# New durations in the planner that spreads side jobs over a stream of matrix products

## The chip, the core and the metric

The kernel runs on one core of a Trainium2 chip, in one launch. The metric is the device time of that launch in microseconds. A core has a matrix engine (PE, its weight loads shown apart as PEld), a vector engine (DVE), an activation engine (ACT), a general engine (POOL) and a queue engine (SP) that here only issues DMAs. Each engine works its own instructions in the order in which they stand in its queue, and waits on the others through semaphores.

## The reference, cut to what matters

Two transformer-like blocks over 256 tokens of width 2048, everything in float32. The first has a gated attention of 8 heads with forget gates, and an RWKV-7 recurrence of 16 heads; the second a gated causal convolution, a latent attention with rotary positions of 16 heads, and an attention over 256 memory tokens.

```python
h = rmsnorm(x); u = h @ w_in                      # 2048 -> 12488 columns
o_a = fox_attention(q, k, v, log_f) * silu(z_a)   # 8 heads of 128
o_b = (groupnorm(rwkv7_scan(r, decay, k, v, kk, kk*a)) + bonus) * silu(z_b)
m = sigmoid(g_a) * (o_a @ w_proj_fox) + sigmoid(g_b) * (o_b @ w_proj_rwkv)
x = rmsnorm(x + m @ w_out)
p = rms_norm(x) @ w_in_2                          # second block
o_conv = (b_gate * causal_conv(c_gate * u)) * silu(conv_z) @ w_conv_out
o_mla  = (mla_attention(c_q, c_kv, k_rope) * silu(mla_z)) @ w_mla_out
o_mem  = (memory_attention(mem_q, mem) * silu(mem_z)) @ w_mem_out
out = x + (sigmoid(g_conv)*o_conv + sigmoid(g_mla)*o_mla + sigmoid(g_mem)*o_mem) @ w_o
```

## The kernel before, in words

All large products are written as one stream, group by group: lora, r, kr, vr, fq, fk, fv, fz, zb, then ga with pf, gb, pr, wo for the first block; mk, mv, cq, ckv, krope, mq, mz, the heads' qr, qn, kn, kv, the convolution's cg, cu, cb, cz, then gm with mo, gc with co, lz, gl with lo and w2 for the second. Weights come as blocks of 128 x 1024 float32 through SP's queue. `conv_to` (L399) splits each block: ACT rounds it to a high part (whi), DVE subtracts to get a low part (wlo). Each product is then made of three matmuls: high by high, high by low, low by high. There are 4 buffers for raw blocks and 4 for each part.

A group is either channel-major (the matmul has 256 columns, four accumulators) or token-major (512 columns, two accumulators, `tm=True`). `gemm` (L472) goes through a group in rounds of two blocks; at the head of a round it writes the conversion of two further blocks. A channel-major round is 48 matmuls, a token-major one 24. Accumulators lie in 5 PSUM banks, and the last product of an accumulator is followed by its evacuation.

Everything else is a side job: a Python generator that writes some instructions and yields. `pump` (L459) is called four times in a round, after 12 matmuls of 256 columns or 6 of 512. It lets each of the first three waiting jobs take a step, or up to six steps where the job yields SOFT, as long as the planner doesn't hold DVE or ACT for too busy. For that the helpers keep three clocks, in estimated microseconds: `mm` adds to the clock of PE, `tt`, `ts`, `stt` and others to that of DVE, `act` to that of ACT. A job isn't stepped while DVE's or ACT's clock is over 1.5 us ahead of PE's:

```python
return max(clock["dve"], clock["act"]) > clock["pe"] + pace['m']
```

nor before PE's clock has reached the end of what the job wrote last on DVE or ACT (`Job.waits`, L431). `lag` (L436) holds a job for 5 us of PE's clock, or twice that, while a transfer goes through DRAM: `head_rs` (L597) writes the 8 or 4 rows of a normalisation to DRAM (hd) and reads them back spread over the partitions (hr). `finish` (L447) steps named jobs to their end where their result is needed, whatever the clocks say.

Side jobs that matter here: `rwkv_job` (L819), twice, the second behind the first. It computes the inverse of a triangular matrix by a loop of 31 steps (L956), each a product TM and a sum into W on DVE, whose sizes rise from 31 to 256 elements and fall again; before it a matrix goes through DRAM (Ld, then W1), behind it one comes back as XA, which the matmuls u read. Its last stage scales CE with hr. `fox_job` (L1147), twice, is four attention heads in turn: scores fs, softmax, transposes fpt, products fo. Both of these must be done ahead of ga (`finish(*jf)`, L1226); the RWKV jobs ahead of pr. `mla_job` is the latent attention's heads.

The program is built with `tile.TileContext(nc, schedule_with_timeline_sim=True)`: the order on each engine is laid out when the program is built, so that what is written is not always run in the written order.

Of the kernel before, what the change touches and what calls it, by code (L numbers as in the profile page):

```python
# [11 lines left out]
F32R = mybir.dt.float32r  # L12
# [215 lines left out]
def hybrid_kernel(ctx: ExitStack, tc: tile.TileContext, io, out):  # L228
# [3 lines left out]
    clock = {"pe": 0.0, "dve": 0.0, "act": 0.0}  # L232

    def fsz(ap):
        n = 1
        for s in ap.shape[1:]:
            n *= s
        return n
# [44 lines left out]

    def mm(o, l, r, start=True, stop=True):
        n = fsz(o)
        clock["pe"] += max(0.000424 * n, 0.0001 + 0.0016 * fsz(l) / 2) if l.dtype == F32R else max(0.00168 * n, 0.00168 * fsz(l))
        TE.matmul(o, lhsT=l, rhs=r, start=start, stop=stop)  # L287


# [182 lines left out]
    def gemm(name, pairs, evac):  # L472
# [4 lines left out]
        for b0 in range(0, e["nb"], step):  # L477
# [9 lines left out]
            if e["tm"]:  # L487
                for t in range(2):
                    for b, i, k in ks:
                        wh = hi_t[b][:, i * cols:(i + 1) * cols]  # L490
                        wl = lo_t[b][:, i * cols:(i + 1) * cols]
                        ah = pairs[k // 4][0][:, k % 4, 128 * t:128 * t + 128]
                        al = pairs[k // 4][1][:, k % 4, 128 * t:128 * t + 128]
                        mm(acc[t], ah, wh, start=k == 0, stop=False)
                        mm(acc[t], ah, wl, start=False, stop=False)
                        mm(acc[t], al, wh, start=False, stop=k == kt - 1)
                        if i == per - 1:
                            pump()
                    if ks[-1][2] == kt - 1:
                        evac(t, acc[t])  # L500
            else:
                for c in range(nt):
                    o = acc[c][:, :256]
                    for b, i, k in ks:
                        s = i * cols + 128 * c
                        wh, wl = hi_t[b][:, s:s + 128], lo_t[b][:, s:s + 128]
                        ah, al = pairs[k // 4][0][:, k % 4, :], pairs[k // 4][1][:, k % 4, :]
                        mm(o, wh, ah, start=k == 0, stop=False)
                        mm(o, wh, al, start=False, stop=False)
                        mm(o, wl, ah, start=False, stop=k == kt - 1)  # L510
                    if ks[-1][2] == kt - 1:
                        evac(c, o)
                    pump()
# [1221 lines left out]

MARGIN, SLACK = (1.5, 0), (1.5, 1)
MAXJOBS, NSTEP = 3, 6
CD, CA = 0.065, 0.17
LAG, HOP = 5, 0.0
SOFT = 1  # L1740

# [31 lines left out]
```

## Time and profile before

| | |
|---|---|
| time, median of 3 runs | 2058.05 us (2056.01 to 2065.45) |
| time of the profiled execution | 2055.2 us |
| its span, first to last instruction | 2053.4 us |
| PE busy | 2021.0 us, 98%, 13456 matmuls |
| DVE busy | 1304.9 us, 64%, 1987 instructions |
| ACT busy | 968.3 us, 47%, 1334 instructions |
| POOL busy | 73.9 us, 133 instructions |
| mean granted clock | 0.996 |
| DMA | 374.97 MB, 183 GB/s |

Times of the trace count from the span's start. Matmuls are pipelined: one of 256 columns lasts 0.28 us in the trace while the next starts 0.12 us after it, so its cost is the distance between starts. The granted clock of a stretch is a share of full speed; TensorE runs at one of two levels, 2.4 GHz and half of it, so a stretch at 0.8 has spent two fifths at the lower one.

### The profile page before, as it was taken

Reading aid. Unit: us, or ns where it says so; the run is one execution under the profiler, and the core shown is the slowest. Engines: PE = TensorE matmul, PEld = TensorE weight load, DVE = VectorE, ACT = ScalarE, POOL = GpSimd, SP = SyncE. Lnnn points to the kernel's source line nnn. Section 1 sums busy time; section 2 is a strip of 40 time slices with the busy share of each in tenths; the row PEclk is TensorE's granted clock in tenths of the full one; section 3 lists DMA queues with packets and bytes.
Section 4 is the critical chain, followed back from the end, with each engine's and each line's share of the span. In section 5 each row is a group of like instructions: output and inputs, shape, how many; then the busy total and the mean of one; then the engine's idle time right before and its main releaser. Section 6 shows DMA issues by size and latency. Waiting matters only on the chain.

```text
span 2053.4 us, 33342 instructions
## 1 busy us (share of the span) xinstructions
PE 2021.0 (98%) x13456; PEld 1822.4 (89%) x13456; DVE 1304.9 (64%) x1987; ACT 968.3 (47%) x1334; POOL 73.9 (4%) x133
## 2 busy tenths in 40 slices
PE   8999999998998999999999999999999999999999
PEld 8999989897777888898999999998888889988887
DVE  8776737868446478666865776755755655555554
ACT  6634435444444445554554435445545444444442
POOL 0002000020000000000000000000000000000000
PEclk9999999999999999999999999999999999999999
DMA  7555644544546656665555554556655555566564
GB/s 248 172 182 166 199 131 135 175 134 156 171 155 217 213 191 211 194 209 185 193 188 182 157 175 154 196 164 193 207 185 176 193 172 179 195 212 201 192 195 154
DMA packets 105674, 374.97 MB, mean 183 GB/s; under 512 B 12920, under 2 KB 13904, under 8 KB 105520
## 3 DMA queue, kind: packets, MB, share of 16 engines
q1 hardware_dynamic: 97568, 350.73, 52.8%
q0 software_dynamic: 7952, 22.12, 3.7%
q8 instruction: 105, 1.72, 0.3%
q14 instruction: 49, 0.40, 0.1%
HBM read 365.76 MB, written 5.86 MB: 181 GB/s over the span
## 4 chain that ended last, share of the span: by engine, by line
PE 94%; DMA 2%; DVE 2%; issue 1%; ACT 1%; POOL 0%; SPq 0%; DVEq 0%; ACTq 0%; POOLq 0%
PE acc.lz L287 4%; PE acc.ga L287 4%; PE acc.gb L287 4%; PE acc.gl L287 4%; PE acc.wo L287 4%; PE acc.w L287 4%; PE acc.lo L287 4%; PE acc.gc L287 4%; PE acc.gm L287 4%; PE acc.fq L287 2%; PE acc.r L287 2%; PE acc.zb L287 2%; PE acc.mz L287 2%; PE acc.mq L287 2%; PE acc.fk L287 2%; PE acc.mk L287 2%
## 5 line engine op out<-in xcount | busy, mean ns | idle before, releaser
L242 DVE TENSOR_TENSOR wlo<-raw,whi 128x1024 fp32r<-128x1024 f32 (+1 forms) x659 | 795.7, 1221 | 540.1 <-ACT whi L279 529.9
L279 ACT ACTIVATE whi<-raw 128x1024 fp32r<-128x1024 f32 (+1 forms) x659 | 683.1, 1055 | 757.3 <-issue 88.1
L287 PE MATMUL acc.lz<-h2h,whi 128*128 128x256 f32 x256 | 72.6, 284 | 0.0
L287 PE MATMUL acc.lz<-h2l,whi 128*128 128x256 f32 x256 | 72.6, 284 | 0.0
L287 PE MATMUL acc.lz<-h2h,wlo 128*128 128x256 f32 x256 | 72.5, 283 | 0.0
L287 PE MATMUL acc.gb<-wlo,hh 128*128 128x512 f32 x128 | 50.5, 398 | 6.0 <-DVE wlo L242 6.0
L287 PE MATMUL acc.ga<-whi,hh 128*128 128x512 f32 x128 | 50.9, 402 | 4.5 <-DVE zb L262 4.5
L287 PE MATMUL acc.ga<-whi,hl 128*128 128x512 f32 x128 | 51.2, 400 | 0.0
L287 PE MATMUL acc.ga<-wlo,hh 128*128 128x512 f32 x128 | 50.8, 397 | 0.0
L287 PE MATMUL acc.gb<-whi,hl 128*128 128x512 f32 x128 | 50.3, 397 | 0.0
L287 PE MATMUL acc.gl<-whi,h2h 128*128 128x512 f32 x128 | 50.0, 392 | 0.0
L287 PE MATMUL acc.gl<-wlo,h2h 128*128 128x512 f32 x128 | 50.0, 392 | 0.0
L287 PE MATMUL acc.gc<-whi,h2l 128*128 128x512 f32 x128 | 50.0, 392 | 0.0
L287 PE MATMUL acc.gl<-whi,h2l 128*128 128x512 f32 x128 | 50.0, 392 | 0.0
L287 PE MATMUL acc.w<-wlo,mgh 128*128 128x512 f32 x128 | 50.0, 390 | 0.0
L287 PE MATMUL acc.w<-whi,mgl 128*128 128x512 f32 x128 | 49.9, 390 | 0.0
L287 PE MATMUL acc.gm<-wlo,h2h 128*128 128x512 f32 x128 | 49.9, 391 | 0.0
L287 PE MATMUL acc.gc<-wlo,h2h 128*128 128x512 f32 x128 | 49.9, 391 | 0.0
L287 PE MATMUL acc.gm<-whi,h2l 128*128 128x512 f32 x128 | 49.8, 390 | 0.0
L287 PE MATMUL acc.gb<-whi,hh 128*128 128x512 f32 x128 | 49.6, 397 | 0.0
L287 PE MATMUL acc.wo<-whi,ml 128*128 128x512 f32 x128 | 49.5, 390 | 0.0
L287 PE MATMUL acc.wo<-wlo,mh 128*128 128x512 f32 x128 | 49.5, 389 | 0.0
(627 smaller groups left out, 6192.6 us busy)
## 6 DMA issues: line engine op xcount, KB each, us to landing
raw<-in_W SPq DMA_DIRECT2D x657, 512.0 KB, 4.0
hr<-hd POOLq DMA_DIRECT2D x10, 512.0 KB, 5.6
hr<-hd POOLq DMA_DIRECT2D x12, 256.0 KB, 5.5
xr<-in_xtm POOLq DMA_DIRECT2D x4, 512.0 KB, 6.6
mt<-in_memT POOLq DMA_DIRECT2D x4, 512.0 KB, 6.5
xbd<-x1g POOLq DMA_DIRECT2D x4, 512.0 KB, 3.0
xo<-xbd POOLq DMA_DIRECT2D x4, 512.0 KB, 5.3
out_tm<-xo SPq DMA_DIRECT2D x8, 256.0 KB, 4.2
```

Of the source, the lines that this page charges most:

```text
L242: DVE.tensor_tensor(out=o, in0=a, in1=b, op=op)
L279: ACT.activation(out=o, in_=a, func=f, scale=scale, **kw)
L287: TE.matmul(o, lhsT=l, rhs=r, start=start, stop=stop)
```

## The change

The price of a split matmul becomes a fixed 0.0133 us plus its columns at 2400 a microsecond, at least 0.109; a plain float32 matmul is charged almost as before. The fixed part of a DVE instruction's price rises from 0.065 to 0.15 us; `CD` is used by `tt`, `ts`, `stt`, `vcopy`, `red` and the softmax. ACT's price stays.

```diff
     def mm(o, l, r, start=True, stop=True):
         n = fsz(o)
-        clock["pe"] += max(0.000424 * n, 0.0001 + 0.0016 * fsz(l) / 2) if l.dtype == F32R else max(0.00168 * n, 0.00168 * fsz(l))
+        clock["pe"] += max(PEF + n / 2400.0, 0.109) if l.dtype == F32R else max(n / 600.0, fsz(l) / 1200.0)
         TE.matmul(o, lhsT=l, rhs=r, start=start, stop=stop)
...
 MAXJOBS, NSTEP = 3, 6
-CD, CA = 0.065, 0.17
+CD, CA, PEF = 0.15, 0.17, 0.0133
 LAG, HOP = 5, 0.0
```

## Rows read from the trace of the kernel before

**Rows 1.** The page: busy time, and the chain that ended last, by engine.
```profile
PE 2021.0 (98%) x13456; PEld 1822.4 (89%) x13456; DVE 1304.9 (64%) x1987; ACT 968.3 (47%) x1334; POOL 73.9 (4%) x133
...
PE 94%; DMA 2%; DVE 2%; issue 1%; ACT 1%; POOL 0%; SPq 0%; DVEq 0%; ACTq 0%; POOLq 0%
```

**Rows 2.** Busy time by stretch: PE, PEld, DVE, ACT, POOL, clock, DMA share, GB/s.
```profile
0.00:10.00 10.00, 3.81 (x16) 3.60 (x16) 4.91 (x15) 5.42 (x9) 0.20 (x4) 1.00 0.74 242
250.00:260.00 10.00, 8.39 (x110) 7.97 (x110) 4.63 (x6) 3.55 (x4) 3.91 (x6) 1.00 0.98 243
388.00:406.00 18.00, 14.90 (x110) 14.50 (x109) 17.51 (x27) 5.43 (x8) 0.00 (x0) 0.91 0.40 124
470.00:486.00 16.00, 10.32 (x43) 7.90 (x43) 13.52 (x39) 6.25 (x15) 0.00 (x0) 0.79 0.11 32
625.00:645.00 20.00, 14.02 (x51) 11.03 (x50) 14.96 (x36) 7.60 (x8) 4.06 (x8) 0.83 0.58 180
2045.00:2053.40 8.40, 4.07 (x18) 3.02 (x17) 1.38 (x2) 0.00 (x0) 0.00 (x0) 1.00 0.17 62
```

**Rows 3.** Waits of PE: for whom, us in total, times, longest.
```profile
PE acc.gb L287 <- DVE wlo L242: 6.0, 1, 6.0
PE acc.ga L287 <- DVE zb L262: 4.5, 1, 4.5
PE acc.fz L287 <- DVE wlo L242: 2.3, 1, 2.3
...
PE u L287 <- DMA XA<-Xd: 1.6, 2, 1.0
```

**Rows 4.** Timeline of DVE: start, us, instruction, idle before it and its releaser.
```profile
388.39 1.23 DVE L242 TENSOR_TENSOR KK<-KK,hr 128x1024 f32<-128x1024 f32 x1 [6.67 <-DMA hr<-hd]
...
631.76 1.67 DVE L262 SCALAR_TENSOR_TENSOR CE<-CE,par,hr 128x256 f32<-128x256 f32 x4 [4.59 <-DMA hr<-hd]
```

**Rows 5.** The tile hr: what its users' engines sat idle for, us, times.
```profile
  DMA hr<-hd: 49.6, 15
```

**Rows 6.** The chain that ended last, two pieces: start, us, what.
```profile
1099.95 5.76 PE acc.qr L287 x48
...
1387.77 10.88 PE acc.mo L287 x48
```

**Rows 7.** Timeline of DVE: loops of both RWKV jobs, and a conversion.
```profile
202.01 0.18 DVE L242 TENSOR_TENSOR TM<-W,W 64x31 f32<-64x31 f32 x1
...
246.87 0.17 DVE L242 TENSOR_TENSOR W<-W,TM 64x31 f32<-64x31 f32 x1
...
457.79 0.18 DVE L242 TENSOR_TENSOR TM<-W,W 64x31 f32<-64x31 f32 x1
...
479.20 0.42 DVE L242 TENSOR_TENSOR TM<-W,W 64x255 f32<-64x255 f32 x1
479.65 0.42 DVE L242 TENSOR_TENSOR W<-W,TM 64x255 f32<-64x255 f32 x1
...
485.36 1.20 DVE L242 TENSOR_TENSOR wlo<-raw,whi 128x1024 fp32r<-128x1024 f32 x1
486.50 0.40 DVE L242 TENSOR_TENSOR W<-W,TM 64x252 f32<-64x252 f32 x1
```

**Rows 8.** Timeline of DVE around 470 to 480.
```profile
472.38 0.48 DVE L1462 MEMSET KRl<- 128x512 f32 x1
...
479.99 0.47 DVE L262 SCALAR_TENSOR_TENSOR zb<-acc.zb,par,zb 128x255 f32<-128x255 f32 x1
```

**Rows 9.** Timeline of PE: first and last head of the second attention job.
```profile
422.57 0.92 PE L287 MATMUL fs<-fk,fq 128*128 128x128 f32 x4
...
469.71 0.82 PE L287 MATMUL fs<-fk,fq 128*128 128x128 f32 x4
...
473.87 0.61 PE L1171 MATMUL fpt<-con,sm 128*128 128x128 f32 x3 [0.58 <-DVE sm L256]
475.06 0.94 PE L287 MATMUL fo<-PT,fv 128*128 128x128 f32 x6 [0.58 <-ACT PT L279]
```

**Rows 10.** The chain that ended last, where pr begins.
```profile
724.78 14.51 PE acc.pr L287 x64
```

## The prediction

> **What bounds the kernel.** Read the busy shares of the page first: PE is busy 2021.0 us of 2053.4, DVE 1304.9, ACT 968.3, and the chain that ended last is 94% PE [rows 1]. So the end is set by the product stream, and its 13456 products stay; only the holes in PE can move. The busy time by stretches shows them [rows 2]. In the first 10 us PE misses 6.2 us and behind the last product 4.3; no planner cost reaches these. Of the 32.4 us of idle PE that leaves 21.9. Four places carry 16.4 of it: 1.6 in 250 to 260, 3.1 in 388 to 406, 5.7 in 470 to 486, 6.0 in 625 to 645. In the last three the granted clock is under 1, that is, PE spent part of the stretch at the lower of its two levels after standing idle. Clock deficit times busy time gives what that cost: 0.09 x 14.9 = 1.4 us, 0.21 x 10.3 = 2.2 and 0.17 x 14.0 = 2.4. So 21.9 + 6.0 = 28 us, 1.4% of the span, is all that better spreading could return.
>
> The waits say who made the holes [rows 3]: products of gb and fz waited for wlo on DVE, those of ga for DVE's part in evacuating zb, those of u for a transfer. On DVE two instructions stand out that waited for hr, the broadcast read back from DRAM: 6.67 us at 388 and 4.59 at 632 [rows 4].
>
> **The change, part by part.** It adds and removes no operation. It alters three planner prices, and with them the place in the written program of each step of a side job.
>
> *Products.* A split product of 256 columns is charged 0.1200 instead of 0.1085 us, one of 512 columns 0.2267 instead of 0.2171. The trace has 48 of the first in 5.76 us (0.1200 each) and 48 of the second in 10.88 (0.2267) [rows 6]: the new prices are exact, the old ones 10% and 4% short. The Trainium skill (TensorE: Matmul & The Clock Gate, the part on back-to-back matmuls) states a start-to-start time of N/2.4 GHz plus about 2.5 ns, which is 109 and 216 ns, nearly the old prices; by it the new clock would outrun PE and let in too much side work. The rows disagree, and they decide.
>
> *DVE.* Each instruction is charged 0.15 us instead of 0.065 beside its elements. A wlo of 1024 lasts 1.20 [rows 7]; the new price is 1.217, the old one 1.132. In the doubling loop of the RWKV inverse the next, dependent instruction starts 0.45 us after one of 255 elements [rows 7], against 0.416 new and 0.331 old. But an instruction that didn't depend on that wlo started 1.14 us after it [rows 7], before it had ended: there the new price is 0.08 too high. The Trainium skill (VectorE: DVE Perf Modes, "The DRAIN you can't avoid") says that the next instruction does not start until the pipeline is empty; by it the new price would be right behind a wlo too, and the rounds below 0.12 us fuller. The row shows an overlap, so I count 1.14.
>
> *What a round admits.* A round of channel-major products is 48 products and two blocks to convert. Before, the planner sees 48 x 0.1085 = 5.21 us, takes off 2 x 1.132 = 2.26 and has 2.95 left; a step of the loop (two instructions of some 255 elements) costs 0.66, so 4.5 steps enter. After: 5.76 - 2.43 = 3.33 at 0.83 a step, 4.0 steps. The chip needs 2 x 1.14 + 4.5 x 0.90 = 6.3 us of DVE for 5.76 of PE (110%) before, and 5.9 (102%) after. With 24 products of 512 columns (5.44 us) it is 116% before; after, (5.44 - 2.43) / 0.83 = 3.6 steps and 102%. So in DVE-bound stretches side jobs get 11 to 20% less, and DVE falls less far behind the plan. Where ACT or the rhythm of the pumps limits a job, a pump is worth 10% (4%) more planner time, and it moves on a little sooner.
>
> *ga at 470.* The evacuation of zb reaches DVE only at 479.99, behind the forced attention head and 34 instructions, 17 steps, of the loop since 457.79 [rows 7, 8]. 11% fewer steps in front of it are 1.9 x 0.90 = -1.7 us. At best the whole hole goes (-5.7 - 2.2 = -7.9), at worst none of it.
>
> *Forced heads.* The second attention job has its four heads' scores between 422.57 and 469.71 [rows 9], and the last head is forced by the wait for the job ahead of ga. 12% more on these 47.1 us is 5.7 us, 0.36 of a mean interval of 15.7. A forced head takes from 469.71 to the end of its fo products at 476.00, 6.3 us; 0.36 of it is 2.3. Products of ga stood between its steps, and PE waited only twice 0.58 us in it, but zb's evacuation was held up by all of it: I take half, +1.1 us, between 0 and +6.3.
>
> *Waits counted in planner time.* LAG is 5 planner us. A pump follows 12 products of 256 columns or 6 of 512: 1.30 us before either way, 1.44 or 1.36 after. To reach 5 takes four pumps in all four cases, so the time that hr is given stays. The doubled LAG takes eight pumps before and seven after where the products have 256 columns. That is the read of XA in 250 to 260, for which u already waited 1.6 us [rows 3]: 1.44 us less cover, +1.4 (0 if other products fill it).
>
> *Small waits.* The two of 0.58 us [rows 9], for DVE and ACT, stand for steps that the planner took for done. With the right DVE price I take half off: -0.6 us, between -1.2 and 0.
>
> *The holes at fz and gb* (3.1 + 1.4 and 6.0 + 2.4 = 12.9 us with the clock) come from a DVE that stood for hr while wlo was queued behind. Their cover is unchanged, but all stages shift by some us, and whether blocks already converted carry PE over is a matter of phase: an engine sat idle 15 times for this transfer [rows 5], and only two of them cost PE much. I take 0, between -12.9 (both covered) and +12.9 (two more like them).
>
> Sum: -1.7 + 1.1 + 1.4 - 0.6 + 0 = +0.2 us on the profiled execution's 2055.2, thus 2055.4. That execution lies 2.85 below the median of the runs, 2058.05; beside the median the forecast is 2058.
>
> A cover that the sum uses: the second RWKV job may end some us later for nothing, since its last stage ran at 632 [rows 4] and the products of pr, which wait for it, begin at 724.78 [rows 10].
>
> **Rivals.**
> *Faster.* With 102% instead of 110% conversions run ahead, both waits for hr are bridged (-12.9), and half of the ga hole goes (-3.9): -16.8, 2041 us. For it: the hole at fz lies in a stretch where DVE worked without a pause behind its wait. Against it: 4.59 us at 632 are pure waiting, which no price shortens.
> *Slower.* DVE stands for hr at other places, with the mechanism of gb: conversions queued in order behind the instruction that waits for DRAM, PE out of converted blocks, then the lower clock. A site like gb costs 8.4 us, one like fz 4.5, and it decides as soon as two more sites fall where no converted pair is in stock: +12.9, 2071 us. For it: 49.6 us of idle time ended with hr, most of it hidden [rows 5]. Against it: the hidden sites are hidden at many different phases today.
> *It hardly acts.* The order on an engine isn't the written order: the memset of KRl, written in the rope job of the second block, ran at 472.38 in the middle of the first [rows 8]. If readiness decides rather than written order, little moves: 2058 us, inside the forecast's band.
>
> **How the numbers follow.** A measurement here tells about 0.5%, 10 us, from no change. Forecast and third rival together, within 10 us of 2058: 0.50. Faster rival: 0.26. Slower rival: 0.24. The likeliest case alone spans 2048 to 2068; to leave out no more than 2 in 10, the range reaches just past both rivals, 2040 to 2074.
>
> **What would show it.** Right: the same products and instruction counts; the first loop, 62 instructions from 202.01 to 247 [rows 7], takes about 50 us instead of 45; the four heads lie some 5 us further apart in all; PE's idle time in the middle stays at 15 to 30 us, with a hole near the start of ga. Wrong: under 10 us of it (faster rival); a further stretch with a granted clock under 0.9 behind a wait for hr (slower rival); a loop still at 45 us, or two whole heads behind zb's last product, either of which breaks a step of the sum.

## The result, and the profile after

The changed kernel takes 2039.03 us (median of 4 runs, 2032.58 to 2041.74) against 2058.87 for the kernel before (also 4 runs). The ratio is 0.9892 (95% interval 0.9863 to 0.9921), so it is faster by 1.1%. The forecast was 2058 and the range began at 2040: the time lies just below it, where the faster rival stood (2041). The profiled execution took 2039.05 us and its span is 2037.2; all comparisons of stages below are made between it and the profiled execution of the kernel before.

The page of the changed kernel, busy time and chain, answers to [rows 1]:
```profile
PE 2015.9 (99%) x13456; PEld 1819.3 (89%) x13456; DVE 1305.6 (64%) x1987; ACT 968.6 (48%) x1334; POOL 74.2 (4%) x133
...
PE 94%; DMA 2%; DVE 2%; issue 1%; ACT 1%; POOL 0%; SPq 0%; DVEq 0%; POOLq 0%; ACTq 0%
```
The counts are those of before. PE's idle time fell from 32.4 to 21.3 us and its busy time by 5.1: together the 16.2 us by which the span is shorter. Of the 5.1, some 2.4 are products that no longer ran at the lower clock (busy time multiplied by the clock's deficit, in pieces of 5 us: 6.3 us before, 3.9 after); where the other 2.7 come from isn't shown.

Busy time by stretches of the changed kernel (columns as in [rows 2], with the same stretches, and 350 to 360 added):
```profile
250.00:260.00 10.00, 8.43 (x117) 7.97 (x117) 3.59 (x4) 3.17 (x5) 3.92 (x6) 0.94 0.93 237
350.00:360.00 10.00, 6.52 (x24) 5.01 (x23) 9.17 (x20) 7.76 (x16) 0.00 (x0) 0.89 0.16 52
388.00:406.00 18.00, 17.56 (x142) 16.95 (x142) 17.94 (x28) 7.45 (x10) 0.00 (x0) 1.00 0.55 175
470.00:486.00 16.00, 16.00 (x75) 13.29 (x74) 13.69 (x28) 8.56 (x14) 0.00 (x0) 1.00 0.58 172
625.00:645.00 20.00, 20.00 (x93) 16.63 (x93) 15.13 (x24) 9.46 (x10) 2.42 (x4) 1.00 0.65 200
```
The holes at ga (470) and gb (625) are gone altogether, clock included: PE is busy 16.00 of 16 and 20.00 of 20. The one at 388 has shrunk, and a new one has opened in fv at 350. PE's waits (columns as in [rows 3]) say the same:
```profile
PE acc.fv L287 <- DVE wlo L242: 3.5, 1, 3.5
PE ms L287 <- DVE mq L262: 2.8, 1, 2.8
PE u L287 <- DMA XA<-Xd: 1.6, 2, 1.2
PE acc.mo L287 <- DVE wlo L242: 1.2, 1, 1.2
```
Where the time came from is read from the first product of each group (timeline of PE: start, us, instruction). Before, with pr at 724.78 [rows 10]:
```profile
465.96 0.47 PE L287 MATMUL acc.ga<-whi,hh 128*128 128x512 f32 x1
...
628.81 0.61 PE L287 MATMUL acc.gb<-whi,hh 128*128 128x512 f32 x2
```
And the three of the changed kernel:
```profile
467.73 0.47 PE L287 MATMUL acc.ga<-whi,hh 128*128 128x512 f32 x1
...
619.61 0.39 PE L287 MATMUL acc.gb<-whi,hh 128*128 128x512 f32 x1
...
707.70 0.61 PE L287 MATMUL acc.pr<-whi,obh 128*128 128x512 f32 x2
```
Up to ga the changed kernel is 1.8 us later, from ga to gb it gains 11.0, from gb to pr 7.9, and after pr it gives back 0.9. So the whole gain lies between the start of ga and the start of pr, where the two places are that the prediction had named and, but for 1.7 us, left standing.

**At ga.** DVE of the changed kernel (start, us, instruction): the loop's start, its conversions, and zb's evacuation, where [rows 7, 8] show it before.
```profile
462.23 1.22 DVE L242 TENSOR_TENSOR wlo<-raw,whi 128x1024 fp32r<-128x1024 f32 x1 [0.41 <-ACT whi L279]
463.37 0.18 DVE L242 TENSOR_TENSOR TM<-W,W 64x31 f32<-64x31 f32 x1
463.48 1.21 DVE L242 TENSOR_TENSOR wlo<-raw,whi 128x1024 fp32r<-128x1024 f32 x1
...
467.99 1.23 DVE L242 TENSOR_TENSOR wlo<-raw,whi 128x1024 fp32r<-128x1024 f32 x1 [0.87 <-PE fpt L1171]
...
469.36 1.21 DVE L242 TENSOR_TENSOR wlo<-raw,whi 128x1024 fp32r<-128x1024 f32 x1
...
473.05 0.36 DVE L242 TENSOR_TENSOR W<-W,TM 64x207 f32<-64x207 f32 x1 [0.33 <-DVE TM L242]
473.07 0.06 DVE L559 MEMSET mf<- 128x1 f32 x1
473.33 0.47 DVE L262 SCALAR_TENSOR_TENSOR zb<-acc.zb,par,zb 128x255 f32<-128x255 f32 x1
```
The loop began 5.6 us later and zb's evacuation came 6.7 us sooner, with 9 steps of the loop in front of it instead of 17. Before, no conversion began between the following one and that at 485.36 [rows 7], 17.8 us:
```profile
467.57 1.21 DVE L242 TENSOR_TENSOR wlo<-raw,whi 128x1024 fp32r<-128x1024 f32 x1
```
The last forced head came sooner too. Timeline of PE, first and last head of the second attention job ([rows 9] before):
```profile
411.36 0.82 PE L287 MATMUL fs<-fk,fq 128*128 128x128 f32 x4
...
457.97 0.82 PE L287 MATMUL fs<-fk,fq 128*128 128x128 f32 x4
```
The four heads are 46.6 us apart in all (47.1 before), but all of them lie 10 to 12 us earlier.

**At gb.** DVE's timeline of the changed kernel around CE, which waits for hr ([rows 4] before); hy is what is sent through DRAM:
```profile
632.95 1.22 DVE L242 TENSOR_TENSOR wlo<-raw,whi 128x1024 fp32r<-128x1024 f32 x1
...
634.40 0.43 DVE L242 TENSOR_TENSOR hy<-hy,ht 128x256 f32<-128x256 f32 x1
636.91 1.23 DVE L242 TENSOR_TENSOR wlo<-raw,whi 128x1024 fp32r<-128x1024 f32 x1 [2.08 <-ACT whi L279]
...
638.67 1.22 DVE L242 TENSOR_TENSOR wlo<-raw,whi 128x1024 fp32r<-128x1024 f32 x1
...
642.40 1.22 DVE L242 TENSOR_TENSOR wlo<-raw,whi 128x1024 fp32r<-128x1024 f32 x1 [0.78 <-ACT whi L279]
647.11 1.67 DVE L262 SCALAR_TENSOR_TENSOR CE<-CE,par,hr 128x256 f32<-128x256 f32 x4 [3.48 <-DMA hr<-hd]
...
649.09 1.22 DVE L242 TENSOR_TENSOR wlo<-raw,whi 128x1024 fp32r<-128x1024 f32 x1
```
And the same place before:
```profile
619.23 1.22 DVE L242 TENSOR_TENSOR wlo<-raw,whi 128x1024 fp32r<-128x1024 f32 x1
...
623.77 0.42 DVE L242 TENSOR_TENSOR hy<-hy,ht 128x256 f32<-128x256 f32 x1
...
634.14 1.22 DVE L242 TENSOR_TENSOR wlo<-raw,whi 128x1024 fp32r<-128x1024 f32 x1
```
The wait itself hardly changed, 4.59 us before and 3.48 after. What changed is what stands around it: three conversions between hy and CE instead of none, and so 6.7 us without a conversion instead of 14.9. The waits for hr are as many as ever: the engines that use it stood idle for it 48.3 us in 16 places (49.6 in 15 before, [rows 5]).

### The profile page after: what moved, and what is told of

Same layout as the page of the kernel before. It is cut to its first block, busy times and chain, and to the rows that moved or that the text cites. A ratio compares the mean times of both kernels' runs of the same rounds, so it can differ in the third digit from the quotient of the medians.

```text
span 2037.2 us, 33332 instructions
## 1 busy us (share of the span) xinstructions
PE 2015.9 (99%) x13456; PEld 1819.3 (89%) x13456; DVE 1305.6 (64%) x1987; ACT 968.6 (48%) x1334; POOL 74.2 (4%) x133
## 4 chain that ended last, share of the span: by engine, by line
PE 94%; DMA 2%; DVE 2%; issue 1%; ACT 1%; POOL 0%; SPq 0%; DVEq 0%; POOLq 0%; ACTq 0%
PE acc.lz L287 5%; PE acc.ga L287 4%; PE acc.gl L287 4%; PE acc.wo L287 4%; PE acc.w L287 4%; PE acc.gb L287 4%; PE acc.lo L287 4%; PE acc.gc L287 4%; PE acc.gm L287 4%; PE acc.fq L287 2%; PE acc.vr L287 2%; PE acc.mz L287 2%; PE acc.cb L287 2%; PE acc.fk L287 2%; PE acc.mk L287 2%; PE acc.mq L287 2%
## 5 line engine op out<-in xcount | busy, mean ns | idle before, releaser
L287 PE MATMUL acc.gm<-whi,h2h 128*128 128x512 f32 x128 | 49.6, 391 | 0.0
L287 PE MATMUL acc.w<-whi,mgh 128*128 128x512 f32 x128 | 49.5, 391 | 0.0
L287 PE MATMUL acc.wo<-whi,mh 128*128 128x512 f32 x128 | 49.3, 395 | 0.0
```

## The experiments

**One price alone, and each half of the program.** Theory: DVE's price had been too low, so that steps were written ahead of what DVE can do, and zb's evacuation and the conversions stood behind them. Rivals: the product price does it; or the two holes fall anew with any shift of phase.

```diff
# pe_only: the change, but
+CD, CA, PEF = 0.065, 0.17, 0.0133
# dve_only: the kernel before, but
+CD, CA = 0.15, 0.17
# first_part: both new prices up to the finish(*jf) ahead of ga, then the old ones
# last_part: the old ones up to there, then both new ones
```


> New product prices (0.1200 and 0.2267 us), DVE price as before (0.065). Theory 1, product price: a pump is worth 10% more planner time, so attention heads move on sooner, the last head's scores come near 458 us instead of 470, and both holes (470 to 486, 628 to 636) go: about 2039 to 2043 us. Theory 2, DVE price: cheap DVE steps still crowd the loop in front of zb's evacuation, the hole near 470 stays: 2050 to 2060 us. Theory 3, phase: any alteration moves the holes about, and the time lies anywhere from 2035 to 2065.

> New DVE price (0.15), product prices as before. Theory 1: heads are not sooner, rather later, since DVE looks fuller while PE's clock is still slow; the hole near 470 stays or grows: 2058 to 2070 us. Theory 2: fewer loop steps stand in front of zb's evacuation, the holes shrink: 2040 to 2048 us. Theory 3: anywhere from 2035 to 2065.

> All new prices up to the forced end of the attention jobs ahead of ga, the old ones from there on. If the state in which the jobs reach ga decides both holes: 2039 to 2043 us. If the hole ahead of gb depends on the prices used during ga and pf: the hole near 470 goes and the one near 630 stays, about 2050 us. If what comes behind 640 us matters, more than 3 us away from both.

> Old prices up to the forced end of the attention jobs ahead of ga, the new ones from there on. If the state at ga decides: 2056 to 2060 us, with the hole near 470 as before. If the prices during ga and pf decide the second hole: about 2050 us, the hole near 470 there and the one near 630 gone.

Measured: pe_only 2096.37 us (ratio 1.0196, 1.0178 to 1.0215), dve_only 2052.86 (0.9977, 0.9966 to 0.9988), first_part 2045.97 (0.9945, 0.993 to 0.996), last_part 2058.74 (1.0002, 0.999 to 1.0015). The product price alone costs 37 us, so that rival is gone; the time lies outside every range that had been set for it (2035 to 2065). DVE's price alone gains some 5 us, a quarter of the change, and misses the theory's 2040 to 2048: by itself it isn't the cause either, and its heads came later (428.8 to 480.3). PE's waits in pe_only:
```profile
PE acc.zb L287 <- DVE zb L262: 12.0, 1, 12.0
PE acc.ga L287 <- DVE wlo L242: 8.1, 1, 8.1
```
DVE there ran 15 products TM of the loop, with their sums, from 451.88 to 463.85 in one piece, and zb's first evacuation only behind them, at 464.21.

The halves take the gain apart. With the new prices only ahead of ga, the ga hole closes (no wait, 2046); with them only behind it, both holes stay (2059). So neither half alone closes the gb hole, and in particular not the prices that hold while gb runs. In first_part it is even wider. DVE's timeline there (the lines are shifted by 4) has no conversion for 16.2 us:
```profile
623.32 1.22 DVE L246 TENSOR_TENSOR wlo<-raw,whi 128x1024 fp32r<-128x1024 f32 x1
637.14 1.67 DVE L266 SCALAR_TENSOR_TENSOR CE<-CE,par,hr 128x256 f32<-128x256 f32 x4 [5.85 <-DMA hr<-hd]
...
639.52 1.22 DVE L246 TENSOR_TENSOR wlo<-raw,whi 128x1024 fp32r<-128x1024 f32 x1
```

**How much DVE price, and two edits without any price.**
```diff
# cd11 and cd20: the change with
+CD, CA, PEF = 0.11, 0.17, 0.0133    # cd20: 0.20
# old_lag8: the kernel before, head_rs holds for 8 planner us
-        yield from lag()
+        yield from lag(8)
# old_loop1: the kernel before, one step of the loop a pump
-            yield SOFT
+            yield
```


> New product prices, DVE price 0.11. By the sum of a round (2 conversions and loop steps of two instructions of 255 elements): 4.5 steps enter, DVE needs 110% of the products' time, as much as before the change. Crowding theory: the time depends on that ratio (122% gave 2096 us with the product price alone, 110% is before, 102% is after, 92% with the DVE price alone gave 2053), so about 2050 to 2065 us here. Phase theory: no order among the ratios, anywhere from 2035 to 2095.

> New product prices, DVE price 0.20: 3.5 steps enter, DVE needs 94% of the products' time. Crowding theory: no DVE queue, but side jobs fall behind and heads are forced ahead of ga as with the DVE price alone (92%): 2045 to 2056 us. Phase theory: anywhere from 2035 to 2095.

> The kernel before, but the normalisations that read hr back from DRAM wait 8 planner us instead of 5 (seven pumps instead of four, some 4 us more). If the holes at 390 and 630 come from too short a cover of this transfer, DVE no longer stands for hr there and both holes shrink: 2043 to 2050 us, the hole at 470 stays. If they come from a DVE queue that is too full, the instruction still arrives ahead of the conversions: 2054 to 2062 us.

> The kernel before, but the loop of the RWKV inverse yields plainly: one step per pump and only when DVE's clock allows it, instead of up to six. If the loop's crowding makes the hole near 470, that hole shrinks under 2 us and the time is 2048 to 2053 us, with the hole near 630 as before. If the forced attention head makes it, the hole stays: 2056 to 2062 us.

Measured: cd11 2047.21 (0.9933, 0.9917 to 0.9949), cd20 2040.38 (0.9906, 0.9891 to 0.9921), old_lag8 2045.82 (0.9934, 0.9916 to 0.9951), old_loop1 2051.15 (0.9952, 0.9935 to 0.9969). Both prices ran faster than the theory of a crowded DVE had it (2050 to 2065 and 2045 to 2056): charging DVE too much cost nothing at 0.20. The longer lag helped, but not where it was meant to: the idle time for hr stayed at 48.7 us and gb still waited 4.2; the heads came at 412.1 instead of 422.57, and zb's evacuation at 472.94 instead of 479.99. One step a pump closed the ga hole with no price changed, but not by slowing the loop: the first one took 44.9 us, as before; the second began at 478.14 instead of 457.79, behind zb's evacuation at 472.54.

**A rule from these, and forecasts by it.** Loop steps that the planner lets into a round, (48 products - 2 conversions) / (2 small instructions) in its own prices, put the six kernels with changed or unchanged prices in a rough order: fastest at 3.5 to 4.0 (the two at 4.5 lie 12 us apart). Three theories were set against each other: this number decides (A), the product price must be right too (B), phase (C). At the same time the two hand edits were joined, and the lag was added to the change.
```diff
# dve10: the kernel before, but
+CD, CA = 0.10, 0.17
# cd22: the change, but
+CD, CA, PEF = 0.22, 0.17, 0.0133
# new_lag8: the change with lag(8) in head_rs
# old_both: the kernel before with lag(8) and the plain yield
```


> The old product price with a DVE price of 0.10. Loop steps that the planner lets into a round are (48 x product price - 2 x (1.067 + CD)) / (2 x (0.266 + CD)). By kernel that ran so far: 5.3 steps 2096 us, 4.5 steps 2047 (new product price, 0.11), 4.5 steps 2059 (before), 4.0 steps 2039 (after), 3.5 steps 2040 (0.20), 3.3 steps 2053 (DVE price alone, 0.15). Here it is (5.21 - 2.33) / 0.73 = 3.9 steps. Theory A, the time follows this one number with a valley at 3.5 to 4: 2038 to 2043 us, without any change of the product price. Theory B, the product price must be right too, since pumps and LAG count in it: 2048 to 2058, like the DVE price alone. Theory C, no such rule holds and each price just shifts the phase: anywhere between 2040 and 2060, with holes at other places than in any kernel so far.

> The new product price with a DVE price of 0.22: (5.76 - 2.57) / 0.97 = 3.3 steps a round, as many as with the DVE price alone, which ran in 2053. Theory A (the number of steps sets it): 2047 to 2056 us. Theory B (product price right, DVE price anything from 0.15 up): 2038 to 2043. Theory C (phase): either, with the wait for hr at a place that none of the other kernels had.

> The changed kernel with 8 instead of 5 planner us held for the read back of hr. It still has 48.3 us of idle DVE that ended with hr, and holes of PE at 350 to 360 (3.5 us, clock 0.77), 400 to 410 and 645 to 650. Theory that the wait for hr is what is left: DVE's idle time for hr falls below 20 us, the hole in fv closes, and the time falls by 4 to 8 us to 2031 to 2035. Rival, that those waits are hidden now and more lag only makes the RWKV and normalisation chains later: 2037 to 2043, no gain.

> Old prices, with both hand edits: 8 planner us held for hr, and one step of the loop a pump. Apart they took off 12.8 us (lag) and 9.9 (loop). If both act on the same hole, that at ga, the two together give what the better one gives, 2043 to 2048. If they act on two different holes (ga by the loop, fz and gb by the lag) they add: 2034 to 2038, at or below the changed prices. If the loop's slower pace pushes the RWKV chain's last stage into gb, a new hole there: 2050 to 2056.

Measured: dve10 2038.89 (0.9899, 0.9879 to 0.9918), cd22 2050.08 (0.995, 0.9929 to 0.997), new_lag8 2040.26 (0.9907, 0.9876 to 0.9938), old_both 2047.74 (0.994, 0.9919 to 0.9961). Both forecasts of A came out, and B fell (C allowed cd22's time and missed dve10's by 1 us): with the product price left wrong, a DVE price of 0.10 gives all of the gain. The Trainium skill (TensorE: Matmul & The Clock Gate, the part on back-to-back matmuls) states N/2.4 GHz plus about 2.5 ns between the starts of products, with no weight loads counted, which gives 109 and 216 ns, nearly the old prices; the trace has 120 and 227 [rows 6]. By these runs it doesn't matter which of the two is charged, so long as DVE's price fits it. The lag gives the change nothing (the idle time for hr went up to 56.6 us), and the two hand edits don't add.

**Which price, and does it have to be true?**
```diff
# wlo_only: the kernel before, conversions charged 0.17 us more
+                clock["dve"] += 0.17
                 sub(lo_t[j][:, p], raw_t[j][:, p], hi_t[j][:, p].bitcast(F32))
# scaled: the change with both prices too high
+CD, CA, PEF = 0.204, 0.17, 0.0233
# cd13: the change with
+CD, CA, PEF = 0.13, 0.17, 0.0133
```


> Old prices, and only the conversion wlo is charged 0.17 us more (1.302 instead of 1.132); steps of side jobs keep their old price. Loop steps that the planner lets into a round: (5.21 - 2 x 1.302) / 0.662 = 3.9. Theory A, that the time follows how much side work a round lets in, whatever price does it: 2037 to 2045 us, as with the changed prices (4.0 steps, 2039) and with a DVE price of 0.10 (3.9 steps, 2039). Rival, that the price of the small instructions is what counts, since forced heads and norms have dozens of them: no more than a third of the gain, 2050 to 2058.

> Both prices wrong together: a product of 256 columns at 0.130 (the trace has 0.120) and a DVE price of 0.204. Steps a round (6.24 - 2 x 1.271) / (2 x 0.470) = 3.9. Theory A: 2037 to 2045. Rival, that the prices have to be those of the trace: at least 8 us slower than the changed kernel, 2047 to 2060.

> The new product price with a DVE price of 0.13: (5.76 - 2 x 1.197) / (2 x 0.396) = 4.25 steps, between the changed kernel's 4.0 (2039) and 4.5 (2047, and 2059 before). Theory A as a smooth valley: 2039 to 2046. Rival, that each price only shifts the phase: 2048 to 2058 is as likely as 2036 to 2048.

Measured: wlo_only 2048.77 (0.995, 0.993 to 0.997), scaled 2041.4 (0.9924, 0.9897 to 0.995), cd13 2039.44 (0.9913, 0.9892 to 0.9935). Prices 8% above the trace's for the products, with DVE's raised to match, do as well as the true ones; scaled and cd13 came out as A had it. wlo_only missed: A had 2037 to 2045. In it the ga hole is closed as A said, but gb waited 6.6 us:
```profile
617.84 1.22 DVE L242 TENSOR_TENSOR wlo<-raw,whi 128x1024 fp32r<-128x1024 f32 x1
631.11 1.67 DVE L262 SCALAR_TENSOR_TENSOR CE<-CE,par,hr 128x256 f32<-128x256 f32 x4 [5.29 <-DMA hr<-hd]
...
633.10 1.22 DVE L242 TENSOR_TENSOR wlo<-raw,whi 128x1024 fp32r<-128x1024 f32 x1
```
So A doesn't explain the place at gb. For this the traces of all kernels so far were laid side by side. The loss of a stretch is its length less PE's busy time multiplied by the granted clock, summed over pieces of 5 us; the distance is the longest from the start of one wlo to the start of the second next, which is how long DVE goes on with one conversion in between. Times are medians; losses and distances are read from the one profiled execution of each kernel.

| kernel | steps a round | time, us | loss 410 to 490 | distance 490 to 720 | loss 490 to 720 |
|---|---|---|---|---|---|
| after | 4.0 | 2039.0 | 0.0 | 10.5 | 0.0 |
| cd11 | 4.5 | 2047.2 | 3.8 | 12.9 | 1.4 |
| dve10 | 3.9 | 2038.9 | 0.0 | 13.0 | 1.4 |
| scaled | 3.9 | 2041.4 | 0.0 | 13.0 | 2.3 |
| old_loop1 | - | 2051.2 | 1.2 | 13.3 | 4.2 |
| cd20 | 3.5 | 2040.4 | 1.2 | 13.7 | 3.1 |
| old_both | - | 2047.7 | 0.0 | 13.9 | 5.1 |
| cd22 | 3.3 | 2050.1 | 3.8 | 14.3 | 5.7 |
| cd13 | 4.25 | 2039.4 | 0.6 | 15.9 | 6.4 |
| old_lag8 | 4.5 | 2045.8 | 5.4 | 15.9 | 7.2 |
| new_lag8 | 4.0 | 2040.3 | 0.0 | 16.6 | 6.9 |
| last_part | both | 2058.7 | 7.4 | 17.3 | 8.2 |
| before | 4.5 | 2058.9 | 7.6 | 17.5 | 8.6 |
| wlo_only | 3.9 | 2048.8 | 0.0 | 17.9 | 9.6 |
| first_part | both | 2046.0 | 0.0 | 18.5 | 10.0 |
| dve_only | 3.3 | 2052.9 | 4.1 | 19.1 | 9.6 |
| pe_only | 5.3 | 2096.4 | 15.9 | 35.3 | 22.5 |

Three things stand in it. First, the loss between 410 and 490 is 0 to 1.2 us with 3.5 to 4.25 steps a round, 3.8 to 7.6 at 4.5 and 15.9 at 5.3. The 4.1 and 3.8 us at 3.3 steps, and the 1.2 of old_loop1 and cd20, aren't at ga: they lie before 440, and from 445 to 490 these kernels lose nothing. What orders the loss at ga can be counted in the traces, in these kernels and in the two that follow: the steps of the second loop that DVE ran ahead of the first of zb's last four evacuations.

| steps ahead of zb's evacuation | kernels | loss 445 to 490 |
|---|---|---|
| 0 to 9 | 13, after (9) and first_part (9) among them | 0.0 |
| 15 | cd13 | 0.6 |
| 17 | before, last_part, old_lag8 | 7.6, 7.4, 5.4 |
| 20 | cd11 | 3.8 |
| 31 | pe_only | 15.2 |

Second, the loss at gb doesn't follow the steps a round: among the kernels with 3.5 to 4.25 steps it goes from 0 to 9.6. But it rises with the distance, roughly as the distance less 8 to 13 us. Two rounds of 24 products of 512 columns, all that four buffers of converted blocks hold, last 2 x 5.44 = 10.9 us by [rows 6]. The distance is the single longest one and the loss is that of the whole stretch, which in some kernels (cd20, cd22, dve_only, new_lag8) comes from two places.

Third, the two columns aren't the whole time: cd11 loses 5.1 us in both places and cd13 7.0, yet cd11's traced execution is 5 us longer. Nor is the time fixed by the program: the executions of one kernel differ by 3 to 14 us (wlo_only took 2041 to 2043 three times and 2049 to 2052 four times; new_lag8 took 2036 to 2047 and was traced at 2046.9), as much as the gb hole costs. Whether that hole comes and goes between executions of one program isn't shown, since each has one trace.

**What makes such a stretch?** Bursts of side steps that the planner lets in, or waits which stand in DVE's queue whatever the prices are.
```diff
# margin05: the change, jobs held at 0.5 us instead of 1.5
+MARGIN, SLACK = (0.5, 0), (1.5, 1)
# nstep2: the change, at most two steps of a job a pump
+MAXJOBS, NSTEP = 3, 2
```


> The changed kernel; in the first half a job is held when DVE's or ACT's clock is over 0.5 us ahead of PE's, instead of 1.5. In the 17 kernels so far PE's loss (idle time and lower clock) between 490 and 720 rises with the longest time that DVE takes from one wlo to the second next: 10.5 us gives 0, 13 gives 1 to 2, 14 gives 3 to 6, 16 gives 6 to 7, 17.5 gives 8 to 9, 18.5 gives 10. In the changed kernel the longest is 10.5 there but 15.1 at 341, where PE loses 8 us. Theory, that bursts of side work between conversions make the holes: the smaller margin cuts bursts by 1 us, the longest distances shrink to at most 12 and the time falls to 2030 to 2036. Rival, that forced heads and waits for the read back of hr make the long stretches, which no margin shortens: 2037 to 2050, with at least one distance of 14 or more. In either case the relation of loss to distance between 490 and 720 should hold.

> The changed kernel with at most two steps of a job at a pump instead of six. The loop then gets up to 8 steps a round, which the clocks hold to 4.0 anyway; only bursts of more than two steps go. Theory of bursts: distances of at most 12, 2030 to 2036. Rival (forced heads and waits for hr): 2037 to 2050, and the relation of loss to distance holds.

Measured: margin05 2046.04 (0.9936, 0.9916 to 0.9957), nstep2 2036.68 (0.9894, 0.9872 to 0.9917). The relation held for both: nstep2 has a distance of 11.2 us between 490 and 720 and no loss there, margin05 one of 20.8 and a loss of 11.2. That bursts make the stretches did not hold for margin05, which got slower; nstep2 stayed under the 12 us that this theory had set, but so had the changed kernel (10.5). The longest stretch of margin05, in DVE's timeline:
```profile
636.54 1.23 DVE L242 TENSOR_TENSOR wlo<-raw,whi 128x1024 fp32r<-128x1024 f32 x1 [1.05 <-ACT whi L279]
640.47 0.29 DVE L266 COPY SV<-sa 64x128 f32<-64x128 f32 x1 [2.70 <-ACT SV L279]
641.10 0.29 DVE L266 COPY SV<-sa 64x128 f32<-64x128 f32 x1 [0.34 <-ACT SV L279]
643.39 1.29 DVE L242 TENSOR_TENSOR ycl<-AR,ych 128x512 fp32r<-128x512 f32 x2 [2.00 <-ACT ych L279]
647.89 1.23 DVE L242 TENSOR_TENSOR sql<-SQ,sqh 128x1024 fp32r<-128x1024 f32 x1 [3.20 <-ACT sqh L279]
...
654.71 1.23 DVE L242 TENSOR_TENSOR wlo<-raw,whi 128x1024 fp32r<-128x1024 f32 x1
```
Here DVE stands four times for ACT, in the last stages of the RWKV job, and not for hr at all; 7.1 of the 11.2 us are lost here. nstep2 had forecasts of 2030 to 2036 and 2037 to 2050 and fell between; with its interval it can't be told from the change. No version was found that is surely faster than the changed kernel: dve10, cd13, cd20, scaled, new_lag8 and nstep2 all lie within 2.4 us of it.

## Why the prediction was wrong, step by step

**What bounds the kernel** was right: the same products, only holes can go, and 28 us is all there is; 16.2 came.

**"What a round admits"** is the step that failed first: it took the planner's own count for what DVE does, and counted every step of the loop at the 0.90 us of the largest. The first loop, said to stretch from 45 to 50 us, took 44.7, which the prediction had named as a sign of being wrong. Timeline of the changed kernel, the loop's first instruction, one of its conversions and the copy behind its last step ([rows 7] before: 202.01, and the last pair at 246.87):
```profile
201.48 0.18 DVE L242 TENSOR_TENSOR TM<-W,W 64x31 f32<-64x31 f32 x1 [0.96 <-DMA W<-Ld]
...
209.65 1.23 DVE L242 TENSOR_TENSOR wlo<-raw,whi 128x1024 fp32r<-128x1024 f32 x1 [0.87 <-ACT whi L279]
...
246.18 1.11 DVE L266 COPY W<-W 64x1024 f32<-64x1024 f32 x1
```
31 steps in 45 us are 7.8 rounds of 5.76, 4.0 steps a round, in both kernels. DVE wasn't over-full either, neither at 110% before nor at 102% after: from 202 to 247 it was busy 38.3 of 45 us before and 38.7 after, with PE busy all of it; a step took 0.66 us on average (20.57 us for 31 before), and eight times in these eight rounds DVE waited for ACT's whi, as in the line at 209.65. So the prices don't slow the loop: over all 19 kernels, with 3.3 to 5.3 planned steps a round, the first one took 41 to 46 us. What moved is its start, from 199 us (pe_only) to 219 (cd22). What holds the pace at about 4 steps isn't shown.

**"Forced heads"** had the wrong sign. It let the attention job lose 12% of its steps and come 5 us later. It came 10 to 12 us sooner: the last head's scores lie 9.8 us ahead of ga's first product instead of 3.8 behind it. Why it came sooner isn't shown; a longer lag alone brought it as early (412.1 in old_lag8). The forecast counted how many steps are admitted and not when they come.

**"ga"** is one of the two terms that broke the sum: -1.7 us, of at most -7.9, where all 7.6 us of loss went (table). It counted 11% fewer steps of the loop in front of the evacuation, and held the order for fixed. The loop began later and the evacuation sooner, which left 9 steps of 17; in every kernel with so few the loss at ga is nothing.

**"The holes at fz and gb"** is the other and the larger one: held at 0 with bounds of 12.9 to either side, it measured -7.0. At fz part of it moved: 388 to 406 is nearly whole, and fv has a hole of 3.5 us at 350. By the same measure of loss, 250 to 410 went from 6.5 to 8.1 us. At gb all 8.6 went. The working said that hr's cover is unchanged because it is counted in pumps, and the wait for hr indeed is much the same. But the wait isn't the cost: the cost is the time in which DVE converts nothing, and that depends on whether conversions stand between hy and CE. The kernels with 3.5 to 4.25 steps a round show that this falls either way (0 to 9.6 us), so "a matter of phase" was the right word for gb and 0 its wrong middle: the kernel before had a bad phase already, and a new draw was more likely to gain than to lose (of the other 18 kernels 13 lose less there). That the changed kernel loses nothing at all there is, as far as these runs show, luck.

**"Waits counted in planner time"** and **"Small waits"** missed by little: u waited 1.6 us for XA as before, where +1.4 had been added (the clock of 250 to 260 fell to 0.94, some 0.5 us), and both waits of 0.58 us went, where half was taken off.

In sum, by the measure of loss: +0.2 us ahead of 250, +1.6 from 250 to 410, -7.6 from 410 to 490, -8.6 from 490 to 720 and +0.9 behind it, so -13.5; the other 2.7 of the 16.2 us stay unexplained.

**Right**: the second RWKV job could end later without harm (CE ran at 647.11 instead of 631.76 and pr began sooner), and the faster rival named the holes at ga and gb and the time within 2 us. The time was luck in part: it took 12.9 us off at fz and gb, where 7.0 came, and halved the ga hole, which went whole. Its reason, conversions that run ahead at 102% of DVE, isn't borne out: wlo_only, new_lag8 and cd13 let in as few steps and lose 6.4 to 9.6 us at gb.

What stays open: why the phase at gb is good in one kernel and bad in the next, and so why this change closed the hole there. The distance tells which it is from the trace afterwards; no run forecast it from prices. A long distance and idle PE can also feed each other, since conversions wait for buffers that PE frees; in the quoted stretches that cost PE time DVE was at its own work or waited for hr or ACT, and for PE at most 0.6 us; in the longest one, pe_only's 35.3 us, it waited 6.8 us for products of PE.

## What to carry to other kernels

In a planner that spreads work, the prices count against each other: the product price corrected alone cost 37 us here, DVE's alone gained 5, both together 20, and both set too high cost nothing that could be measured. A right ratio wasn't enough, though: wlo_only had it and gained 9. To judge a hole, don't look at the wait alone but at the queue around it: here PE lost time where the engine that feeds it went longer than about two rounds with only one feeding instruction in between. Where a stage's cover is left to phase, look at whether the present draw is a good or a bad one before setting its change at nothing.

## What the hardware showed that wasn't expected

The waits for the DRAM round trip did not shrink when the program left more room for it. With 8 instead of 5 planner us the idle time for hr was 48.7 us against 49.6 (kernel before) and 56.6 against 48.3 (after); over all kernels it was 48 to 62 us, and it doesn't order the times: dve10 has 56.2 at 2039 us, the kernel before 49.6 at 2059.
